# Low parts last: reordering the products of a split-precision trunk step on one Trainium2 core

## The chip, the cores and the metric

The kernel runs on one core of one Trainium2 chip. The metric is the device time of one execution in microseconds; smaller is better. Six instruction streams matter. PE (TensorE) multiplies matrices; PEld, its weight load, is listed beside it. DVE (VectorE), ACT (ScalarE) and POOL (GpSimd) work on elements. SP (SyncE) issues most of the DMAs, and POOL issues those that accumulate into their destination.

## The reference, cut to what matters

One step of a decoder layer for 512 prompt positions and 8 sample positions (520 columns in all), model width 1024, everything in float32:

```
h = x + 0.5 * swiglu(rms_norm(x), gate1, up1, down1)          # first FFN, 2816 wide
proj = rms_norm(h) @ w_in                                     # -> pool input, z, x/B/C, dt
pool_out = windowed means of the pool input, mixed by w_pool
y = ssd_scan(silu(conv(x/B/C)), dt)                           # 4 chunks of 128 positions, 16 heads
y = group_norm((y + d_skip * x) * silu(z)) * ssd_norm         # 2 groups of heads
h = h + concat(pool_out, y) @ w_out                           # 1536 -> 1024
h = h + 0.5 * swiglu(rms_norm(h), gate2, up2, down2)          # second FFN
out = rms_norm(h)
```

For the 8 samples the scan is one step from a given state: the new state is the old one times a decay plus an outer product, and the sample's output needs, for each of 16 heads, the old state multiplied by the C row and summed over its 128 columns. That sum is called a **readout** here.

## The kernel before, in words

**Split precision.** A float32 matmul is replaced by three faster ones. Every weight tile and every activation tile is held as a high part (rounded) and a low part (the rest): w = whi + wlo, x = xhi + xlo, and w·x is taken as whi·xhi + whi·xlo + wlo·xhi. The helper mm3 (L145) issues these three for one block of 128 rows: L146 (whi, xhi), L149 (whi, xlo), L150 (wlo, xhi). A product over 512 or 1024 rows is 4 or 8 calls of mm3 that accumulate into one PSUM bank. So the low weight is used by the third matmul of a product already.

**Making the parts.** load_unit (L140) loads a raw weight by SP's queue; split (L129) makes the high part by an ACT cast (L134) and the low part by a DVE subtraction, raw minus high (L136). The other way is part_by_dma (L230): ACT casts the high part, ACT writes its negative into the low tile (L232), and a DMA from POOL's queue adds the raw weight from DRAM (L233). In the second FFN the load of a tile does the same in L380 to L382, and the quarter of a tile that the code calls qs goes through part_by_dma. Raw tiles, high and low tiles and PSUM banks rotate through a few buffers, so an early release of one lets a later load begin.

**The FFNs** (class Ffn). A fast scheme forms a block of outputs from seven products instead of eight; each product (method product, L448) is four mm3 calls (j = 0 to 3) into a bank called A or BE. Tiles whose names begin with Down are the down projection in the same scheme, and their activations are called gs. The first matmul of a product is pinned in program order; everything else is placed by a list scheduler that simulates the program when the kernel is built (L1405) and fixes the order of each engine's instructions.

**The mixer.** Its order is written out by hand as strings: CONV_PLAN, GATE_PLAN, LAST_PLAN (L41 to L48), in which a letter is a stage and a number its argument. In GATE_PLAN: z are eight units of the z projection; A and B are the two halves of one scan block (numbers 0 to 7: four chunks for each of two head groups); s is a number of sample readouts; G(g) (gate, L1249) multiplies head group g by silu(z), and needs that group's readouts; H(g) (gate_out, L1261) squares the result on ACT, sums the squares on DVE (L1268), sums over partitions on PE into psr_y (L195), takes root and reciprocal, and writes the normalised activations catg (L1276 to L1278). o, g, h (wout, L1232) are the units of the out projection for the pooled part, head group 0 and head group 1: four units each, with four mm3 calls for each of four banks, and DVE adds each bank to h (L1243).

A sample readout (sample, L1088) covers one sample and one group of heads: SP loads a C row (cb, L1090) and a 128 x 4 x 128 state (h0, L1092, four buffers), DVE multiplies them (L1094, pinned), and four ACT instructions with an accumulator output (L1097, pinned) sum 128 columns each. There are 16 of them. The states themselves are updated later, during the second FFN (L1139 to L1143).

Of the kernel before, what the change touches and what calls it, by code (L numbers as in the profile page):

```python
# [13 lines left out]
ALU = mybir.AluOpType  # L14
# [8 lines left out]
HB = NT // 2  # L23
HALVES = (slice(0, HB), slice(HB, NT))
KD = D // P
# [9 lines left out]
CHUNKS = (8, 8, 6)  # L35
LOW_ON_DVE = ((2, 0), (3, 0), (KF - 1, 1))
ON_ACT = 4
STATES = ((1, 1, 1, 1), (6, 17, 19, 20, 21), 4)
LOW_BY_DMA = {1: (2, 3, 4, 5, 6), 2: (*range(7), 9, 11)}

CONV_PLAN = (  # L41
    "b0 b1 d0 b2 b3 x0 x1 v0 d1 x2 x3 d2 X0 p0 y0 c0 A0 k0 p1 x4 m0 x5 B0 c1 p2 m1 A1 x6 c2 A2 B1 x7 X1 m2 A3"
)
GATE_PLAN = (
    "z0 B2 A4 z1 B3 p3 s1 z2 B4 s2 z3 c3 A5 s2 s2 z4 m3 B5 s2 A6 z5 e0 s2 G0 z6 A7 s2 z7 B6 s2 o0 H0 o1 B7 s1 G1 o2 "
    "o3 g0 g1 H1 g2 g3"
)
LAST_PLAN = "h0 h2 h1 n0 h3 n1 n2 n3"  # L48
# [15 lines left out]
def tile_trunk_step(ctx: ExitStack, tc: tile.TileContext, ins: dict, outs: dict):  # L64
    nc = tc.nc
# [6 lines left out]
    wp = ctx.enter_context(tc.tile_pool(name="wp", bufs=3, side="right"))  # L72
    tmp = ctx.enter_context(tc.tile_pool(name="tmp", bufs=2, side="right"))
    dr = ctx.enter_context(tc.tile_pool(name="dr", bufs=1, space=DRAM))
    ps = [None]
# [5 lines left out]
    vec = vx[:, :NVEC]  # L81
    h = vx[:, NVEC:].rearrange("p (d t) -> p d t", d=KD)
# [62 lines left out]
    def mm3(ps, whi, wlo, xhi, xlo, start, stop, pin=False, **kw):  # L145
        first = nc.tensor.matmul(ps, whi, xhi, start=start, stop=False, **kw)  # L146
        if pin:
            tc.keep_in_program_order(first)
        nc.tensor.matmul(ps, whi, xlo, start=False, stop=False, **kw)  # L149
        nc.tensor.matmul(ps, wlo, xhi, start=False, stop=stop, **kw)  # L150

    def ws(w, k, m=P):
        return w[:, k * m : (k + 1) * m]
# [76 lines left out]
    def part_by_dma(hi, lo, s, home):  # L230
        nc.scalar.copy(hi, s)
        nc.scalar.activation(out=lo, in_=hi.bitcast(F32), func=AF.Copy, scale=-1.0)  # L232
        nc.gpsimd.dma_start(out=lo, in_=home, accum_op=ALU.add)  # L233
# [22 lines left out]
    class Ffn:  # L256
# [175 lines left out]
        def quarter(self, f):  # L432
# [7 lines left out]
            if len(src.shape) == 3:  # L440
                h, l = (t.rearrange("p (j c) -> p j c", j=4) for t in (hi, lo))
            if f in LOW_BY_DMA[self.i] and (f, 1) not in LOW_ON_DVE:
                part_by_dma(h, l, src, self.dram[f][1][:, 512:])
# [4 lines left out]
        def product(self, f, p):  # L448
            js = range(KD // 2)
            if f not in self.A:  # L450
                self.load(f, *self.behind.get(f, ((), (), False)))
                n = f"{self.i}_{f}"
                self.A[f] = ps[0].tile([P, 512], F32, tag="A", bufs=2, name=f"A{n}")
                self.BE[f] = ps[0].tile([P, 2, 512], F32, tag="BE", bufs=2, name=f"BE{n}")
                self.ac[f] = [self.wx.tile([P, 2, HB], F32, tag="ac", bufs=3, name=f"ac{n}_{q}") for q in range(2)]
            if p != 1 and 4 not in self.w[f]:
                self.quarter(f)
            slot, dst, opens = {1: (0, 0, True), 2: (1, 1, True), 5: (3, 2, True), 6: (5, 0, False),
                                3: (2, 2, False), 7: (4, 0, False), 4: (6, 0, False)}[p]
            opens = opens and (p != 2 or f in self.whole)  # L460
            out = self.A[f] if dst == 0 else self.BE[f][:, dst - 1]
            (whi, wlo), k = self.w[f][p]
            xth, xtl = self.nx[:2]
            for j in js:
                if isinstance(f, int):
                    x = xth[:, j, slot], xtl[:, j, slot]
                else:
                    x = (self.gs[f.c * CHUNKS[0] // 2 + j][:, q, {5: 6, 6: 5}.get(slot, slot)] for q in range(2))
                mm3(out[:, :HB], ws(whi, k[j]), ws(wlo, k[j]), *x, opens and j == 0,
                    j == KD // 2 - 1, pin=j == 0 and (self.i == 1 or f != 1), skip_group_check=True)  # L470
            a, c = self.ac[f]
            if p == 1 and f not in self.whole:
                a = self.BE[f][:, :, :HB]
            keep = {1: a[:, 0], 6: a[:, 1], 7: c[:, 0], 5: c[:, 1]}.get(p)
            if keep is not None:
                self.copied = nc.scalar.copy(keep, out[:, :HB]).ins  # L476
                if (f, p) == (2, 7):
                    self.tail = self.copied
            if p == 7:
                nc.vector.tensor_tensor(out=c[:, 0], in0=c[:, 0], in1=c[:, 1], op=ALU.add)  # L480
# [53 lines left out]
        def stream(self, before, last_chunk):  # L534
# [6 lines left out]
            for t in tiles:  # L541
                for _ in range(STATES[0][t.d] if not isinstance(t, int) else t in STATES[1]):
                    next(self.states, None)
# [68 lines left out]
        def down_by_half(self, c, lo, after, wd):  # L612
            n = KF - lo
            banks, units = {}, []
            for d in range(KD):
                if d < STATES[2]:
                    next(self.states)
# [104 lines left out]
    nx2, xa = [], []  # L722
# [51 lines left out]

    ps[0] = tc.alloc_tile_pool(name="ppm", bufs=8, space=PSUM, reuse_waits="tile")
    mixer(tc, ins, outs, dict(locals()))
    f2["xg"].release()
    xa[0].release()
# [69 lines left out]
def mixer(tc, ins, outs, e):  # L848
    nc = tc.nc
    cst, act, wp, tmp, dr, pool = (e[x] for x in ("cst", "act", "wp", "tmp", "dr", "pool"))  # L850
    ones, queued, squared = e["ones"], e["queued"], tuple(e["added"])
    bank, load_unit, mm3, ws, v, rstd, rstds, vec, h, nx2, raw_tile, open_f2, fin, fill = (
        e[x] for x in ("bank", "load_unit", "mm3", "ws", "v", "rstd", "rstds", "vec", "h", "nx2", "raw_tile",
                       "open_f2", "fin", "fill"))
    xh, xl, _, r = nx2[0]
    xa = e["xa"][0]
# [194 lines left out]
    ysm = mp.tile([P, NX, NS], F32, tag="ysm", name="ysm")  # L1051
# [4 lines left out]
    def rows_bc(b, a, g):  # L1056
        return scr_bc.rearrange("b (a g n) -> b a g n", a=2, g=2)[b, a, g].unsqueeze(0).to_broadcast([P, P])
# [27 lines left out]
        nc.vector.tensor_tensor(out=sxdt[:, gs], in0=sdt[:, gs], in1=X[:, gs, SEQ:NT], op=ALU.mult)  # L1085


    def sample(b, g):  # L1088
        cb = tmp.tile([P, HB], F32, tag="ta", name=f"cb{b}{g}")[:, :P]
        nc.sync.dma_start(out=cb, in_=rows_bc(b, 1, g))  # L1090
        h0 = mp.tile([P, 4, P], F32, tag="h0", bufs=4, name=f"h0_{b}{g}")
        nc.sync.dma_start(out=h0, in_=ins["state_ssm"][:, b, 4 * g : 4 * g + 4])  # L1092
        tc.keep_in_program_order(
            nc.vector.tensor_tensor(out=h0, in0=h0, in1=cb.unsqueeze(1).to_broadcast([P, 4, P]), op=ALU.mult))  # L1094
        for q in range(4):
            tc.keep_in_program_order(
                nc.scalar.activation(out=junk, in_=h0[:, q], func=AF.Copy,  # L1097
                                     accum_out=ysm[:, 4 * g + q, b : b + 1]))
# [131 lines left out]
            nc.vector.tensor_tensor(out=zbox[0][:, j, hs], in0=bs[b][:, :HB], in1=r[:, hs], op=ALU.mult)  # L1230

    def wout(cat, j, d2, fin=None):  # L1232
        wh, wl = load_unit(ins["w_out"][j, d2], 1024, f"wo{j}{d2}", behind.get((j, d2), ()))
        for d in (2 * d2, 2 * d2 + 1):
            for b, hs in enumerate(HALVES):
                if d != 1 or j != 2:
                    ps = bank(f"wo{j}_{d}{b}")
                else:
                    ps = e["ps"][0].tile([P, 512], F32, tag="A", bufs=2, name=f"wo{j}_{d}{b}")
                for k in range(4):  # L1240
                    i = (d % 2) * 4 + k
                    mm3(ps[:, :HB], ws(wh, i), ws(wl, i), cat[:, 0, k, hs], cat[:, 1, k, hs], k == 0, k == 3)
                nc.vector.tensor_tensor(out=h[:, d, hs], in0=ps[:, :HB], in1=h[:, d, hs], op=ALU.add)  # L1243
                if fin is not None:
                    fin(d, b, hs)

    cats, behind = {}, {}
# [35 lines left out]

    smp = [(b, g) for g in range(2) for b in range(NS)]

    def samples(n):
        for _ in range(n):
            if smp:
                sample(*smp.pop(0))

    pooled, box = [], {}

    def ssd(c):
        return c % NC, c // NC

    def outs_a():
# [14 lines left out]
        "c": lambda j: pooled[j][0](),  # L1311
        "m": lambda j: pooled[j][1](),
        "s": samples,
        "A": lambda j: ssd_a(*ssd(j)),
        "B": lambda j: ssd_b(*ssd(j)),
        "z": zproj,
        "o": lambda j: wout(catp, 0, j),
        "G": gate,
        "H": gate_out,
        "g": lambda j: wout(cats[0], 1, j),  # L1320
        "h": lambda j: wout(cats[1], 2, j, fin),
        "n": fill,
        "e": lambda j: outs_a(),
# [101 lines left out]
```

## Time and profile before

| | us |
|---|---|
| three runs of the kernel | 962.70, 962.92 (median), 964.66 |
| the profiled execution | 963.72 |
| its span, first to last instruction | 961.9 |
| PE busy / DVE busy / ACT busy / POOL busy | 945.5 / 852.3 / 641.2 / 144.9 |

The mean granted clock of TensorE was 0.996. By stage, on the profile's clock: the first FFN runs to about 355 us, the mixer from there to about 615 (in it the out projection from 526 to 611, its last units mixed with the start of the second FFN), the second FFN to 942, the final norm to the end.

How to read a row of the timeline: start and duration in us, engine, line of the kernel, operation, output tile, an arrow, the input tiles, the shapes, the count; in brackets the idle time of the engine before it and what ended that. A matmul's own duration (0.28 us) is longer than its distance from the next one, because they overlap in the array. A row of waits gives the waiting engine, tile and line, what it waited for, the total in us, how often, and the longest. A row of stretches gives the stretch, its length, and then the busy time (and the number of instructions) of PE, PEld, DVE, ACT and POOL, the granted clock, the share of the DMA engines and GB/s.

### The profile page before, as it was taken

How to read it: one execution, taken by the hardware profiler on the slowest of the kernel's cores; microseconds unless marked ns; L12 is line 12 of the kernel's file. 1: busy time of each engine (PE TensorE's matmuls, PEld its weight loads, DVE VectorE, ACT ScalarE, POOL GpSimd, SP SyncE). 2: the span in 40 equal slices, each digit the busy share in tenths (PEclk: the TensorE clock that was granted, in tenths of full speed). 3: DMA queues.
4: the chain of work that ended last, by engine and by line, in shares of the span. 5: the costliest groups of instructions: out<-in, count | busy, mean ns of one | idle time of the engine just before them, and what ended most of it. 6: DMA issues, size and time to landing. Idle time of an engine off the chain costs nothing. (4 is left out here: it accounts for less than half of the span.)

```text
span 961.9 us, 19663 instructions
## 1 busy us (share of the span) xinstructions
PE 945.5 (98%) x7652; PEld 926.2 (96%) x7652; DVE 852.3 (89%) x1460; ACT 641.2 (67%) x1208; POOL 144.9 (15%) x228
## 2 busy tenths in 40 slices
PE   9999999999999999999999999999999999999996
PEld 8999999999999999999999999999999999999995
DVE  6999899998988788779979998898889999989886
ACT  7777756677566455485688645777776676766763
POOL 0011100001000001046252000112112101122120
PEclk9999999999999999999999999999999999999998
DMA  7665553455544243363355323457666646666642
GB/s 210 181 166 149 142 165 112 123 147 141 159 123 115 87 133 101 93 195 117 111 157 166 108 89 121 110 126 171 166 154 188 160 126 155 174 176 175 185 144 90
DMA packets 53629, 137.29 MB, mean 143 GB/s; under 512 B 7640, under 2 KB 15768, under 8 KB 53536
## 3 DMA queue, kind: packets, MB, share of 16 engines
q1 hardware_dynamic: 39840, 104.18, 33.6%
q0 software_dynamic: 13424, 31.73, 17.2%
q8 instruction: 60, 0.98, 0.4%
q14 instruction: 33, 0.27, 0.1%
q10 hardware_dynamic: 272, 0.13, 0.0%
HBM read 128.67 MB, written 7.34 MB: 141 GB/s over the span
## 5 line engine op out<-in xcount | busy, mean ns | idle before, releaser
L476 ACT COPY ac<-A 128x260 f32<-128x260 f32 x85 | 31.7, 373 | 34.7 <-PE A L150 33.5
L412 DVE TENSOR_TENSOR s<-raw 128x1024 f32<-128x1024 f32 x39 | 47.6, 1220 | 3.6 <-DMA raw<-in_w2gu 2.5
L476 ACT COPY ac<-BE 128x260 f32<-128x260 f32 x41 | 15.4, 376 | 30.0 <-PE BE L150 29.0
L146 PE MATMUL inx<-xh_mx,whi_inx 128*128 128x260 f32 x112 | 31.8, 284 | 0.0
L149 PE MATMUL inx<-xl_mx,whi_inx 128*128 128x260 f32 x112 | 31.6, 282 | 0.0
L150 PE MATMUL inx<-xh_mx,wlo_inx 128*128 128x260 f32 x112 | 31.6, 282 | 0.0
L977 DVE SCALAR_TENSOR_TENSOR A<-U,h,A 128x544 f32<-128x544 f32 x36 | 28.8, 799 | 1.1 <-ACT A L975 0.7
L295 PE MATMUL P<-x,raw 128*128 128x260 f32 x128 | 28.9, 387 | 0.0
L295 PEld LDWEIGHTS P<-x,raw 128*128 128x128 f32 x128 | 24.6, 193 | 4.0 <-DMA raw<-in_w1gu 0.3
L146 PE MATMUL wo<-catg,whi_wo 128*128 128x260 f32 x96 | 27.6, 287 | 0.0
L134 ACT CAST thi<-raw 128x1024 fp32r<-128x1024 f32 (+1 forms) x14 | 14.2, 1012 | 20.0 <-PE wo L149 9.9
L150 PE MATMUL wo<-catg,wlo_wo 128*128 128x260 f32 x96 | 27.2, 283 | 0.0
L149 PE MATMUL wo<-catg,whi_wo 128*128 128x260 f32 x96 | 27.1, 282 | 0.0
L1097 ACT ACTIVATE junk<-h 128x128 f32<-128x128 f32 x64 | 19.7, 308 | 7.9 <-DVE h L1094 6.5
L150 PE MATMUL A<-xth_f,qs 128*128 128x260 f32 x84 | 24.0, 286 | 0.9 <-DMA qs<-in_w2gu 0.8
L1139 ACT ACTIVATE so<-br,sxdt 128x128 f32<-128x128 f32 x64 | 22.5, 375 | 3.3 <-DVE room L1141 3.1
L146 PE MATMUL A<-xth_f,qs 128*128 128x260 f32 x84 | 23.9, 284 | 0.0
L149 PE MATMUL A<-xtl_f,qs 128*128 128x260 f32 x84 | 23.7, 282 | 0.0
L237 DVE TENSOR_TENSOR gs<-gq,gs 128x780 fp32r<-128x780 f32 (+1 forms) x28 | 23.2, 829 | 0.4 <-ACT gs L236 0.4
L146 PE MATMUL inz<-xh_mx,whi_inz 128*128 128x260 f32 x80 | 22.9, 287 | 0.0
L149 PE MATMUL inz<-xl_mx,whi_inz 128*128 128x260 f32 x80 | 22.7, 284 | 0.0
L150 PE MATMUL inz<-xh_mx,wlo_inz 128*128 128x260 f32 x80 | 22.6, 283 | 0.0
(2530 smaller groups left out, 4747.3 us busy)
## 6 DMA issues: line engine op xcount, KB each, us to landing
raw<-in_w2gu SPq DMA_DIRECT2D x44, 512.0 KB, 4.2
raw<-in_w1gu SPq DMA_DIRECT2D x41, 512.0 KB, 4.1
raw<-in_w_in SPq DMA_DIRECT2D x24, 512.0 KB, 3.6
raw<-in_w1d SPq DMA_DIRECT2D x16, 512.0 KB, 4.3
raw<-in_w2d SPq DMA_DIRECT2D x16, 512.0 KB, 4.6
raw<-in_w_out SPq DMA_DIRECT2D x12, 512.0 KB, 3.6
ab<-scr_acs SPq DMA_DIRECT2D x8, 512.0 KB, 4.5
h<-in_state_ssm SPq DMA_DIRECT2D x16, 256.0 KB, 3.5
```

Source lines behind the costliest of these rows:

```text
L134: cast = nc.scalar.copy(h, src)
L146: first = nc.tensor.matmul(ps, whi, xhi, start=start, stop=False, **kw)
L149: nc.tensor.matmul(ps, whi, xlo, start=False, stop=False, **kw)
L150: nc.tensor.matmul(ps, wlo, xhi, start=False, stop=stop, **kw)
L237: low = nc.vector.tensor_tensor(out=lo, in0=s, in1=hi.bitcast(F32), op=ALU.subtract)
L295: mm = nc.tensor.matmul(self.banks[f, u][b][:, :HB], ws(self.raw[f][:, u], j + 4 * q), xg[:, slot[q]], start=j == q == 0, stop=j == 3 and ...
L412: nc.vector.tensor_tensor(out=s1, in0=diag, in1=up0, op=ALU.add)
L476: self.copied = nc.scalar.copy(keep, out[:, :HB]).ins
L977: nc.vector.scalar_tensor_tensor(out=A[:, :n], in0=U[:, j : j + n], scalar=w(j), in1=A[:, :n], op0=ALU.mult, op1=ALU.add)
L1097: nc.scalar.activation(out=junk, in_=h0[:, q], func=AF.Copy, accum_out=ysm[:, 4 * g + q, b : b + 1]))
L1139: nc.scalar.activation(out=o[:, q], in_=br, func=AF.Copy, scale=sxdt[:, j, b : b + 1]))
```

## The change

Four edits.

1. A new helper, mm_low_last, issues for one product all whi·xhi and whi·xlo matmuls first (eight of a product of twelve) and the four wlo·xhi behind them. The products of the second FFN's tiles and all out units use it; the first FFN, the in projection and the last down projection keep mm3.
2. The low parts of the out units g0 and g1 (OUT_LOW_BY_DMA) are made by part_by_dma instead of a DVE subtraction.
3. The first four sample readouts (r2, r2) are summed by one DVE reduction each instead of four ACT instructions.
4. In GATE_PLAN the readouts stand earlier: two instead of one after p3, and the last one, which stood between B7 and G1, is gone from there. B7 goes ahead of o1.

```diff
+OUT_LOW_BY_DMA = ((1, 0), (1, 1))
 GATE_PLAN = (
-    "z0 B2 A4 z1 B3 p3 s1 z2 B4 s2 z3 c3 A5 s2 s2 z4 m3 B5 s2 A6 z5 e0 s2 G0 z6 A7 s2 z7 B6 s2 o0 H0 o1 B7 s1 G1 o2 "
+    "z0 B2 A4 z1 B3 p3 r2 z2 B4 r2 z3 c3 A5 s2 s2 z4 m3 B5 s2 A6 z5 e0 s2 G0 z6 A7 s2 z7 B6 s2 o0 H0 B7 o1 G1 o2 "
     "o3 g0 g1 H1 g2 g3"
 )
...
+    def mm_low_last(ps, whi, wlo, xhi, xlo, start, pin=False, **kw):
+        for k, w in enumerate(whi):
+            for x in (xhi[k], xlo[k]):
+                mm = nc.tensor.matmul(ps, w, x, start=start, stop=False, **kw)
+                if pin:
+                    tc.keep_in_program_order(mm)
+                start = pin = False
+        for k, w in enumerate(wlo):
+            nc.tensor.matmul(ps, w, xhi[k], start=False, stop=k == len(wlo) - 1, **kw)
...
@@ product
+            if self.i == 2:
+                mm_low_last(out[:, :HB], wh, wl, *xs, opens, pin, skip_group_check=True)
+            else:
+                for j in js:
+                    mm3(out[:, :HB], wh[j], wl[j], xs[0][j], xs[1][j], opens and j == 0, j == js[-1],
+                        pin=pin and j == 0, skip_group_check=True)
...
@@ sample
+        if reduce:
+            tc.keep_in_program_order(
+                nc.vector.tensor_reduce(out=ysm[:, 4 * g : 4 * g + 4, b], in_=h0, axis=mybir.AxisListType.X, op=ALU.add))
+            return
...
@@ wout
-        wh, wl = load_unit(ins["w_out"][j, d2], 1024, f"wo{j}{d2}", behind.get((j, d2), ()))
+        src, name = ins["w_out"][j, d2], f"wo{j}{d2}"
+        if (j, d2) in OUT_LOW_BY_DMA:
+            raw = raw_tile(name)
+            nc.sync.dma_start(out=raw, in_=src)
+            wh, wl = e["weight_homes"](1024, name, wp, 3, ("whi", "wlo"))
+            e["part_by_dma"](wh, wl, raw, src)
+        else:
+            wh, wl = load_unit(src, 1024, name, behind.get((j, d2), ()))
...
-                for k in range(4):
-                    i = (d % 2) * 4 + k
-                    mm3(ps[:, :HB], ws(wh, i), ws(wl, i), cat[:, 0, k, hs], cat[:, 1, k, hs], k == 0, k == 3)
+                i = range((d % 2) * 4, (d % 2) * 4 + 4)
+                mm_low_last(ps[:, :HB], *([ws(w, k) for k in i] for w in (wh, wl)),
+                            *([cat[:, q, k, hs] for k in range(4)] for q in range(2)), True)
...
+        "r": lambda n: samples(n, True),
```

More of the change, by code (lines that the diff above doesn't have):

```diff
@@ L463, in product @@
             xth, xtl = self.nx[:2]
[L464 to L470, printed above, removed]
+            if isinstance(f, int):
+                xs = [[x[:, j, slot] for j in js] for x in (xth, xtl)]
+            else:
+                u = {5: 6, 6: 5}.get(slot, slot)
+                xs = [[self.gs[f.c * CHUNKS[0] // 2 + j][:, q, u] for j in js] for q in range(2)]
+            wh, wl = ([ws(w, k[j]) for j in js] for w in (whi, wlo))
+            pin = self.i == 1 or f != 1
+            if self.i == 2:
[4 more added lines that the diff above has]
+                        pin=pin and j == 0, skip_group_check=True)
             a, c = self.ac[f]
@@ L851, in mixer @@
     ones, queued, squared = e["ones"], e["queued"], tuple(e["added"])
-    bank, load_unit, mm3, ws, v, rstd, rstds, vec, h, nx2, raw_tile, open_f2, fin, fill = (
-        e[x] for x in ("bank", "load_unit", "mm3", "ws", "v", "rstd", "rstds", "vec", "h", "nx2", "raw_tile",
+    bank, load_unit, mm3, mm_low_last, ws, v, rstd, rstds, vec, h, nx2, raw_tile, open_f2, fin, fill = (
+        e[x] for x in ("bank", "load_unit", "mm3", "mm_low_last", "ws", "v", "rstd", "rstds", "vec", "h", "nx2", "raw_tile",
                        "open_f2", "fin", "fill"))
@@ L1085, in sample_x, with sample @@
         nc.vector.tensor_tensor(out=sxdt[:, gs], in0=sdt[:, gs], in1=X[:, gs, SEQ:NT], op=ALU.mult)
-    def sample(b, g):
+    def sample(b, g, reduce):
         cb = tmp.tile([P, HB], F32, tag="ta", name=f"cb{b}{g}")[:, :P]
@@ L1232, in wout @@
     def wout(cat, j, d2, fin=None):
-        wh, wl = load_unit(ins["w_out"][j, d2], 1024, f"wo{j}{d2}", behind.get((j, d2), ()))
+        src, name = ins["w_out"][j, d2], f"wo{j}{d2}"
[4 more added lines that the diff above has]
+            e["part_by_dma"](wh, wl, raw, src)
+        else:
+            wh, wl = load_unit(src, 1024, name, behind.get((j, d2), ()))
         for d in (2 * d2, 2 * d2 + 1):
@@ L1284, in mixer, with samples @@
     smp = [(b, g) for g in range(2) for b in range(NS)]
-    def samples(n):
+    def samples(n, reduce=False):
         for _ in range(n):
-            if smp:
-                sample(*smp.pop(0))
+            sample(*smp.pop(0), reduce)
     pooled, box = [], {}
```

## The prediction, made before the result was known

> **What bounds the kernel now.** I read the page's busy times first, then the stretches, then the waits of TensorE (PE).
>
> ```profile
> span 961.9 us, 19663 instructions
> PE 945.5 (98%) x7652; PEld 926.2 (96%) x7652; DVE 852.3 (89%) x1460; ACT 641.2 (67%) x1208; POOL 144.9 (15%) x228
> ```
>
> PE is busy for 98% of the span and the matmul count doesn't change, so nothing here can be worth more than the time in which PE stands still: 961.9 - 945.5 = 16.4 us.
>
> ```profile
> 100.00:150.00 50.00, 50.00 (x419) 50.00 (x418) 45.55 (x71) 31.75 (x50) 4.30 (x5) 1.00 0.56 151
> ...
> 480.00:510.00 30.00, 29.92 (x254) 27.82 (x253) 22.87 (x47) 24.77 (x80) 12.36 (x12) 1.00 0.56 167
> 510.00:560.00 50.00, 50.00 (x419) 48.02 (x418) 49.69 (x99) 34.53 (x104) 5.89 (x4) 1.00 0.42 133
> ```
>
> Undisturbed, 419 matmuls take 50 us: one starts every 0.12 us, whatever its own duration says. VectorE (DVE, third pair) is idle for 7.1 us of 480 to 510 and for 0.3 us of 510 to 560: there it runs behind PE and works without a gap. The waits of PE say where that or anything else reaches PE:
>
> ```profile
> PE psr_y L195 <- DVE X L1268: 1.5, 1, 1.5
> PE A_Down(c=0, d=1)_8807 L150 <- DMA wlo_Down(c=0, d=1)a<-in_w2d: 1.4, 1, 1.4
> ...
> PE A L150 <- DMA qs<-in_w2gu: 0.8, 1, 0.8
> ...
> PE A L150 <- DMA qlo_4b<-in_w1gu: 0.6, 1, 0.6
> PE A_Down(c=1, d=2)_10486 L150 <- DMA wlo_Down(c=1, d=2)a<-in_w2d: 0.6, 1, 0.6
> PE A L150 <- DVE slo_17d L136: 0.5, 1, 0.5
> ```
>
> L150 is the matmul that takes the low part of a weight. Four of these waits are for a low part in the second FFN, which the change reorders; qlo_4b is in the first FFN, which it doesn't. psr_y is gate_out(1) waiting for DVE in the mixer. These are the targets.
>
> **The change part by part. Low parts last.** One stall close up:
>
> ```profile
> 708.17 0.28 PE L146 MATMUL A_Down(c=0, d=1)_8807<-gs,whi_Down(c=0, d=1)a 128*128 128x260 f32 x1
> 708.29 0.28 PE L149 MATMUL A_Down(c=0, d=1)_8807<-gs,whi_Down(c=0, d=1)a 128*128 128x260 f32 x1
> 709.94 0.39 PE L150 MATMUL A_Down(c=0, d=1)_8807<-gs,wlo_Down(c=0, d=1)a 128*128 128x260 f32 x1 [1.37 <-DMA wlo_Down(c=0, d=1)a<-in_w2d]
> 710.16 0.28 PE L146 MATMUL A_Down(c=0, d=1)_8807<-gs,whi_Down(c=0, d=1)a 128*128 128x260 f32 x1
> ...
> 751.83 0.28 PE L149 MATMUL A<-xtl_f,qs 128*128 128x260 f32 x1
> 752.19 0.39 PE L150 MATMUL A<-xth_f,qs 128*128 128x260 f32 x1
> ```
>
> The low weight is wanted by the third matmul of the product. The slip is 709.94 - 708.29 - 0.12 = 1.53 us and 0.10 in the step behind it, 1.63 in all, so a wait of the table costs about 0.25 more than it says; 752.19 slips by 0.24 + 0.10 and isn't even listed. Afterwards eight matmuls stand ahead of the first low one instead of two: it is wanted 6 x 0.12 = **0.71 us later**. The number of matmuls, and of changes of weight (8 in 12), stays. Each stall gives at most 0.71: 709.94 (1.63) gives 0.71; qs at 668.9 (0.8 + 0.25) gives 0.71; 752.19 gives all of its 0.34; 842.7 (0.6 + 0.25) and 868.3 (0.5 + 0.25) give 0.71 each if independent. But the chain that ended last goes between these two over a state's DMA and DVE, not over PE:
>
> ```profile
> 844.26 4.05 DMA room<-in_state_ssm
> ```
>
> Time gained at 842.7 doesn't move what 868.3 waits for, so I count the two once. Sum: 0.71 + 0.71 + 0.34 + 0.71 = **2.5 us**; bounds 0.7 (one gain, the others hanging on the same late chain) and 3.2 (all five).
>
> The order has a price at the start of that FFN, where x is late:
>
> ```profile
> 617.18 0.97 DVE L237 TENSOR_TENSOR xtl_f<-xg_f,xth_f 128x780 fp32r<-128x780 f32 x1
> 618.07 1.24 DVE L237 TENSOR_TENSOR xtl_f<-xd_f,xth_f 128x1040 fp32r<-128x1040 f32 x1
> ...
> 618.86 0.28 PE L149 MATMUL A<-xtl_f,whi_1a 128*128 128x260 f32 x1
> ...
> 619.36 0.39 PE L149 MATMUL BE<-xtl_f,shi_1c 128*128 128x260 f32 x1
> ```
>
> DVE delivers x's low parts of the last j at 618.1 (for A) and 619.3 (for BE), and PE takes BE's at once. BE has then done ten of its twelve matmuls, since the low weights of the first three j don't need that x. With all four low ones last it has done seven: 3 x 0.12 = 0.36 us of work no longer lies beside the wait. I charge **+0.4** (bounds 0, if other ready matmuls fill the place, and 0.7, if A loses its three as well). The other products of both FFN stages want x 0.36 us earlier, where no wait of the table is for x: nothing, bound +0.3.
>
> **Out units.** For g0 and g1 the low part leaves DVE; the same stretch shows what waits for it:
>
> ```profile
> 545.64 1.22 DVE L136 TENSOR_TENSOR wlo_wo<-raw,whi_wo 128x1024 fp32r<-128x1024 f32 x1
> ...
> 551.99 1.22 DVE L136 TENSOR_TENSOR wlo_wo<-raw,whi_wo 128x1024 fp32r<-128x1024 f32 x1
> ...
> 554.18 0.69 DVE L1094 TENSOR_TENSOR h<-h,cb 128x512 f32<-128x512 f32 x1
> ...
> 565.22 0.69 DVE L1268 TENSOR_TENSOR X<-X 128x520 f32<-128x520 f32 x1
> ...
> 564.32 0.28 PE L150 MATMUL wo<-catg,wlo_wo 128*128 128x260 f32 x1
> 566.05 1.11 PE L195 MATMUL psr_y<-X,ones 128*128 128x260 f32 x4 [1.45 <-DVE X L1268]
> ```
>
> DVE has no gap from 510 until the L1268 that PE waits for. Out of this stretch go two L136 (1.13 from start to start) and the last sample's L1094 (0.60), which moves up with its two DMAs: 2.9 us. PE stands 566.05 - 564.32 - 0.12 = 1.6 us. So the wait goes, **-1.6**, if DVE doesn't come later to 510; PE's own work is late next. Added are two ACT negations and two POOL DMAs:
>
> ```profile
> 547.25 1.05 ACT L134 CAST whi_wo<-raw 128x1024 fp32r<-128x1024 f32 x1 [1.33 <-PE wo L149]
> ...
> 558.80 0.28 PE L149 MATMUL wo<-catg,whi_wo 128*128 128x260 f32 x1
> ...
> 700.75 1.05 ACT L381 ACTIVATE wlo_Down(c=0, d=1)a<-whi_Down(c=0, d=1)a 128x1024 fp32r<-128x1024 f32 x1
> ...
> 702.10 0.88 POOL L382 DMA_DIRECT2D wlo_Down(c=0, d=1)a<-in_w2d  x1 [11.20 <-ACT wlo_Down(c=0, d=1)a L381]
> ...
> 594.14 0.90 POOL L233 DMA_DIRECT2D qs<-in_w2gu  x1 [53.46 <-DVE h L1243]
> ```
>
> g1's cast at 547.25, a negation of 1.05, and a DMA that in the same form was in PE's hands 709.94 - 702.10 = 7.8 us after its issue: about 557.4. PE starts g1 at 558.7 and wants the low part 0.95 us on, at 559.6. Cost nothing, margin 2.2 us. POOL has 53 us without other work, so nothing queues behind these DMAs; ACT has 15 us free in 510 to 560. Without that cover each us of lateness is a us.
>
> **Samples.** Four readouts leave ACT for DVE:
>
> ```profile
> L1097 ACT ACTIVATE junk<-h x64: 291/310/314, 485.6 to 556.3; 128x128 f32<-128x128 f32 x64
> L1097 ACT ACTIVATION_READ_ACCUMULATOR junk<-h x64: 185/187/197, 485.8 to 556.5; 128x1 f32 x64
> ...
> L199 DVE RECIPROCAL yr<-yr x4: 1720/1748/1779, 538.0 to 569.0; 128x260 f32<-128x260 f32 x4
> ...
> SPq L1092 <- ACT junk L1097: 16.2, 11, 3.9
> ```
>
> ACT loses 16 pairs of at most 0.50 us, 8 us. DVE gets four reductions of 128x512, an operation the trace doesn't have: from 0.60 (the multiply L1094 of that shape, start to start) to 3.4 us (a reciprocal's 1.75 us for 260 elements, scaled). I take 0.60, since a reduction reads the tile once as L1094 does: 2.4 us, and 0.6 for the moved multiply, 3.0 us inside the 7.1 us that DVE idles in 480 to 510. State loads on SP's queue waited 16.2 us for ACT's readouts to free their buffers; that shrinks, and so may DVE's idle time. Cost 0, bound +3.0 on DVE if none of that idle time can be used.
>
> **B7 ahead of o1.** It issues no more, only 5.9 us earlier, at 532.5 when gate_out(0)'s sums are done:
>
> ```profile
> 531.77 0.68 DVE L1215 TENSOR_TENSOR hst<-pst,hst 128x512 f32<-128x512 f32 x1
> ...
> 532.51 0.47 PE L146 MATMUL wo<-catp,whi_wo 128*128 128x260 f32 x1
> ```
>
> The state that it reads is ready at 532.45: nothing, bound +0.7 (one more DVE operation ahead). It lets the gate's DVE work start sooner.
>
> **The sum.** -1.6 - 2.5 + 0.4 = **-3.7 us**. The profiled execution took 963.72 us around its span of 961.9: 960.0. The median of the three runs, 962.92, lies 0.8 below it, so **959.2 us** is predicted.
>
> **Rivals.** (1) The FFN gains don't reach the end: PE arrives earlier, DVE and the DMAs don't, and the stalls reappear one product on. For: DVE is without a gap around several stalls. Against: their chains start at matmuls of the tile before. Time: 962.9 - 1.6 + 0.4 = 961.7. (2) Slower: the reductions make DVE late. They lengthen the gapless stretch that gate_out(1) ends. Per reduction r, DVE comes 4r + 0.6 later less the idle time it can use (0 to 7.1), less 2.9; PE's wait there grows by that much, and the kernel is slower than before once it exceeds the 2.1 us that the second FFN gives. The point is 4r + 0.6 less the usable idle time = 5.0, that is r = 1.1 (none usable) or 2.9 (all). At r = 3.4 and all usable the growth is 4 x 3.4 + 0.6 - 7.1 - 2.9 = 4.2: 962.9 + 4.2 - 2.1 = 965.0. Against: L1094's row. (3) POOL's DMAs starve under a DVE without gaps. If they had to wait for DVE's next pause, at 566, the low parts would land near 573 instead of 557, 13 us after they are wanted: about 962.9 + 13 - 2.1 = 974. Against: the DMA of 702.10 took 0.88 us to issue and 7.8 to land:
>
> ```profile
> 700.00:705.00 5.00, 4.91 (x41) 4.70 (x40) 5.00 (x10) 3.64 (x10) 0.88 (x1) 1.00 0.42 107
> ```
>
> with DVE busy for 5.00 of those 5 us. This is a rule of the Trainium skill ("SBUF — State Buffer", "SBUF: two separate sides"): descriptors that GpSimd writes wait while a VectorE operation holds the port that they share. By that rule it would be 974. The trace doesn't bear it out for these VectorE operations. (4) The scheduler orders the lists anew and the intended order doesn't come out: about 962.9, either way.
>
> **Chances.** Forecast 0.58, (1) 0.18, (2) 0.09, (3) 0.04, (4) 0.11. A measurement can tell 0.2%, 1.9 us, from no change. Faster by more, below 961.0: the forecast, a third of (1), a third of (4): 0.68. Within: 0.17. Slower: 0.15. The low end takes all five stalls, the mixer and no charge: 962.9 - 1.6 - 3.2 - 0.6 (small slips such as 752.19's that no row lists) = 957.5, rounded down to 957.0; the high end goes into (2), at a loss of 0.5 us: 963.4.
>
> **What would show it.** Right: no psr_y wait; first low matmul ninth in its product, the four L150 waits at most their old value less 0.71; a longer wait for xtl_f at 619; reductions of 0.6 to 0.7 us. Wrong: a wait of PE for wlo_wo from in_w_out, a psr_y wait that grows, or as much total waiting in the second FFN with other names.

## The result, and the profile after

| | us |
|---|---|
| before, six runs | 962.81 (959.27 to 964.66) |
| after, six runs | 956.34 (955.96 to 958.85) |
| ratio, 95% interval | 0.9942 (0.9929 to 0.9955) |
| profiled execution, before and after | 963.72, 956.44 |

By the ratio the change takes off 5.6 us (4.3 to 6.8). 959.2 was predicted, from 957.0 to 963.4: the sign holds, the gain is larger, and the median lies 0.7 below the low end; by the ratio, which puts the 962.92 that I started from at 957.3, it lies just inside. One execution of a later kernel, neither, took 5284 us and is left out of its row. In the lines below, every line number behind the new helper has moved: L150 is now L151, and in the new order a high matmul is L156 and a low one L161.

First the page of the changed kernel, its busy times:

```profile
span 954.7 us, 19636 instructions
PE 942.1 (99%) x7652; PEld 925.0 (97%) x7652; DVE 854.0 (89%) x1462; ACT 635.7 (67%) x1178; POOL 148.9 (16%) x230
```

The span is 7.2 us shorter, with as many matmuls. PE's idle time fell from 16.4 to 12.6 us. The other 3.4 us came out of its busy time, which the page gives as 942.1 instead of 945.5 for the same matmuls: the records of neighbours overlap, and a slip that only shortens the overlap isn't idle time. So the idle time that I took as the limit of the gain wasn't one. Second, the waits of PE that the view of the waits lists, but for two at the start and the end of the kernel (for eps 1.1, for sq_last 0.6) that were there before:

```profile
PE BE_Down(c=1, d=1)_10344 L156 <- ACT c_Down(c=1, d=1)_1_10346 L493: 1.3, 1, 1.3
...
PE BE L156 <- ACT BE L493: 0.7, 1, 0.7
```

psr_y is gone, and so are all four waits for a low part in the second FFN. No wait is for a weight any more. Two new ones are for copies that ACT makes (L493). Third, where the stages begin, by the same instructions in PE's timeline. Of before:

```profile
355.91 0.38 PE L195 MATMUL psr_mx<-acc_mx,ones 128*128 128x260 f32 x1
...
607.45 0.28 PE L146 MATMUL A<-xth_f,whi_1a 128*128 128x260 f32 x1
...
942.24 0.38 PE L824 MATMUL psl<-acc_last,ones 128*128 128x260 f32 x1
```

and of after:

```profile
355.13 0.38 PE L206 MATMUL psr_mx<-acc_mx,ones 128*128 128x260 f32 x1
...
604.20 0.28 PE L156 MATMUL A<-xth_f,whi_1a 128*128 128x260 f32 x1
...
935.13 0.38 PE L841 MATMUL psl<-acc_last,ones 128*128 128x260 f32 x1
```

psr_mx begins the mixer, whi_1a the second FFN, and psl comes behind it; each of the two stretches holds as many matmuls after as before (2050 and 2709). The first FFN, whose code is the same, is 0.8 us shorter: the wait for qlo_4b (0.6) isn't there in this execution. With that code unchanged it ends between 354.7 and 356.3 in the profiles of all kernels here. The mixer fell from 251.5 to 249.1 us (2.5), the second FFN from 334.8 to 330.9 (3.9). The three together give 7.1.

Fourth, the stretches of after that answer to those of before (PE, PEld, DVE, ACT, POOL):

```profile
480.00:510.00 30.00, 30.00 (x256) 28.14 (x255) 26.01 (x50) 20.57 (x56) 14.98 (x12) 1.00 0.62 188
510.00:560.00 50.00, 50.00 (x419) 48.02 (x418) 50.00 (x99) 37.66 (x100) 6.86 (x5) 1.00 0.49 136
```

DVE took 3.14 us more in 480 to 510 (26.01 against 22.87) and was still idle for 4.0 of 30. In 510 to 560 it works without a gap as before, but further ahead, as its timeline shows:

```profile
482.04 0.68 DVE L1111 TENSOR_TENSOR h<-h,cb 128x512 f32<-128x512 f32 x1
482.76 0.69 DVE L1114 TENSOR_REDUCE ysm<-h 128x4 f32<-128x512 f32 x1
483.36 1.20 DVE L1111 TENSOR_TENSOR h<-h,cb 128x512 f32<-128x512 f32 x1
...
558.52 0.70 DVE L1296 TENSOR_TENSOR X<-X 128x520 f32<-128x520 f32 x1
...
563.02 1.04 PE L206 MATMUL psr_y<-X,ones 128*128 128x260 f32 x4
```

The reduction takes 0.60 us from its start to the next (482.76 to 483.36), as the multiply of before did. The sum that PE waits for (L1296) is done at 559.2; before it began at 565.22. PE wants it at 563.02: 3.8 us to spare instead of a wait. The low part of an out unit, by DMA from POOL:

```profile
545.30 0.90 POOL L244 DMA_DIRECT2D wlo_wo<-in_w_out  x1 [11.61 <-ACT wlo_wo L243]
549.20 0.85 POOL L244 DMA_DIRECT2D wlo_wo<-in_w_out  x1 [3.00 <-ACT wlo_wo L243]
```

and the same two in the view of the DMAs, with the KB of each and the median us from issue to landing (its last number):

```profile
wlo_wo<-in_w_out POOLq DMA_DIRECT2D x2, 512.0 KB, 5.8
```

Issue takes 0.85 to 0.90 us and landing 5.8, while DVE is busy for 50.00 of 50 us. PE waits for neither.

Last, the product that stood for 1.63 us in the prediction's stall, now:

```profile
695.94 0.88 POOL L393 DMA_DIRECT2D wlo_Down(c=0, d=1)a<-in_w2d  x1 [10.29 <-PE A L161]
...
702.71 1.11 PE L156 MATMUL A_Down(c=0, d=1)_8797<-gs,whi_Down(c=0, d=1)a 128*128 128x260 f32 x8
...
703.65 0.65 PE L161 MATMUL A_Down(c=0, d=1)_8797<-gs,wlo_Down(c=0, d=1)a 128*128 128x260 f32 x4
```

The first low matmul is the ninth, 0.94 us behind the first high one, and doesn't wait. The DMA is issued 6.8 us ahead of the product's first matmul. Before, it was issued at 702.10 and the product began at 708.17, 6.1 ahead. So the low part is wanted 0.7 us later and is also under way 0.7 earlier, together 1.4, a little less than the 1.53 that PE stood there. The rest is the DMA itself, here in before and in after:

```profile
wlo_Down(c=0, d=1)a<-in_w2d POOLq DMA_DIRECT2D x1, 512.0 KB, 7.8
...
wlo_Down(c=0, d=1)a<-in_w2d POOLq DMA_DIRECT2D x1, 512.0 KB, 6.4
```

At 6.4 us it landed at 702.3, ahead of the product's first matmul: in this execution the old order would hardly have waited either. What the order does shows better at the wait for qs at 668.9. That DMA took 8.1 us to land before and 8.2 in after, and PE no longer waits for it:

```profile
656.42 0.86 POOL L244 DMA_DIRECT2D qs<-in_w2gu  x1 [0.49 <-ACT qs L243]
...
664.73 0.71 PE L161 MATMUL A<-xth_f,qs 128*128 128x260 f32 x4
```

PE takes the low part 8.31 us behind the issue. Before, the DMA was issued at 660.73 and PE was ready for the low part at 667.95, 7.22 behind. Of these 1.09 us the order gives 0.71, an earlier issue the rest.

### The profile page after: what moved, and what is told of

The parts are those of the page before. It is cut to its first block, busy times and chain, and to the rows that moved or that the text cites. A ratio compares the mean times of both kernels' runs of the same rounds, so it can differ in the third digit from the quotient of the medians.

```text
span 954.7 us, 19636 instructions
## 1 busy us (share of the span) xinstructions
PE 942.1 (99%) x7652; PEld 925.0 (97%) x7652; DVE 854.0 (89%) x1462; ACT 635.7 (67%) x1178; POOL 148.9 (16%) x230
## 5 line engine op out<-in xcount | busy, mean ns | idle before, releaser
L493 ACT COPY ac<-A 128x260 f32<-128x260 f32 x85 | 31.7, 373 | 37.2 <-PE A L161 18.5
L493 ACT COPY ac<-BE 128x260 f32<-128x260 f32 x41 | 15.4, 377 | 35.2 <-PE BE L161 16.9
L150 PE MATMUL inx<-xl_mx,whi_inx 128*128 128x260 f32 x112 | 31.6, 282 | 0.0
L151 PE MATMUL inx<-xh_mx,wlo_inx 128*128 128x260 f32 x112 | 31.6, 282 | 0.0
L156 PE MATMUL wo<-catg,whi_wo 128*128 128x260 f32 x192 | 27.4, 285 | 0.0
L156 PEld LDWEIGHTS wo<-catg,whi_wo 128*128 128x128 f32 x192 | 24.8, 188 | 0.2
L1271 DVE TENSOR_TENSOR h<-wo,h 128x260 f32<-128x260 f32 x48 | 19.2, 422 | 5.0 <-PE wo L161 4.8
L150 PE MATMUL inz<-xl_mx,whi_inz 128*128 128x260 f32 x80 | 22.7, 284 | 0.0
L151 PE MATMUL inz<-xh_mx,wlo_inz 128*128 128x260 f32 x80 | 22.6, 283 | 0.0
L147 PEld LDWEIGHTS inx<-xh_mx,whi_inx 128*128 128x128 f32 x112 | 21.1, 188 | 0.2 <-issue 0.2
L156 PE MATMUL A<-xth_f,qs 128*128 128x260 f32 x84 | 21.2, 283 | 0.0
L156 PE MATMUL A<-xtl_f,qs 128*128 128x260 f32 x84 | 21.2, 284 | 0.0
L151 PEld LDWEIGHTS inx<-xh_mx,wlo_inx 128*128 128x128 f32 x112 | 21.1, 188 | 0.0
```

What stands on the lines that cost most here:

```text
L156: mm = nc.tensor.matmul(ps, w, x, start=start, stop=False, **kw)
```

## The experiments

**What another execution of before shows.** The kernel before, profiled once more:

> The kernel before, profiled a second time. Theory (a part of the stalls that I summed belongs to the one profiled execution, whose 963.72 us lie above the middle of the runs): psr_y's 1.5 us is there again, since VectorE's work sets it, but the waits for qs and wlo_Down change by up to a us each, and the span is 1 to 3 us shorter. Rival (all seven are fixed by the schedule): the same rows within 0.2 us.

961.71 us, span 959.9. Its waits of PE, the first and last that matter:

```profile
PE psr_y L195 <- DVE X L1268: 1.5, 1, 1.5
...
PE BE_Down(c=0, d=3)_9075 L146 <- ACT BE_Down(c=0, d=3)_9075 L476: 0.6, 1, 0.6
PE A L150 <- DVE slo_17d L136: 0.5, 1, 0.5
PE A_Down(c=1, d=2)_10486 L146 <- ACT c_Down(c=1, d=2)_0_10488 L476: 0.4, 1, 0.4
...
PE A L150 <- DMA qs<-in_w2gu: 0.2, 1, 0.2
```

The wait for psr_y and that for slo_17d, both for DVE, come back to a tenth. The largest wait for a DMA, 1.4 us for wlo_Down, isn't there (the DMA landed after 6.3 us), and that for qs is 0.2 instead of 0.8. This execution's mixer takes 251.6 us as before, its second FFN 333.25, 1.5 less. So the two largest stalls that I counted in the second FFN differ from one execution to the next, and others come in their place: 0.6 and 0.4 us for copies on ACT, of the kind that seemed new in after.

**The two places apart.** ffn2_only keeps the new order for the products of the second FFN alone (no low parts by DMA, the old GATE_PLAN, mm3 in the out units). mixer_only is the changed kernel but for this:

```diff
-            if self.i == 2:
+            if False:
                 mm_low_last(out[:, :HB], wh, wl, *xs, opens, pin, skip_group_check=True)
```

> Only the products of the second FFN take low parts last; the plan, the readouts and the out units are those of before. Theory (two separate gains): the L150 waits of the second FFN go as in the changed kernel, about -3.5 us there, and the psr_y wait of 1.5 us stays: 959.3. Rival 1 (my forecast's size): each stall gives at most 0.71, -2.1: 960.7. Rival 2 (the stalls went because the mixer ends earlier and the scheduler places the loads of the second FFN otherwise): the same number of stalls under other names, 962.5.

> The changed kernel with the old order (high, high, low for each j) in the second FFN's products; the mixer is that of the changed kernel. Theory: no psr_y wait, PE reaches the second FFN about 2.5 us earlier than before and the L150 waits (qs, wlo_Down, slo_17d; about 4.5 us with their slips) are back: 960.0. Rival 2: the L150 waits stay away because the mixer did it: 956.5.

| | us, median | ratio, 95% interval | mixer | second FFN |
|---|---|---|---|---|
| ffn2_only | 959.17 | 0.9977 (0.9963 to 0.9991) | 251.1 | 331.0 |
| mixer_only | 959.75 | 0.9975 (0.9962 to 0.9988) | 250.4 | 332.85 |
| after | 956.34 | 0.9942 (0.9929 to 0.9955) | 249.1 | 330.9 |

(The stages are measured in the profiled executions, between the same three instructions as above.) Each place gives about 0.24%, 2.2 and 2.4 us, and 4.6 in sum; after's 5.6 agrees within the intervals. The rival, that PE's gain in the FFN only shifts the stalls, would have left ffn2_only at the time of before. It falls, by a narrow margin. ffn2_only came out at the 959.3 that its theory had, but as a gain (before ran at 961.65 beside it) its 2.2 us are nearer to the first rival's 2.1, the forecast's size, than to the theory's 3.5. The waits of ffn2_only show what each edit does:

```profile
PE psr_y L206 <- DVE X L1296: 1.5, 1, 1.5
PE BE_Down(c=1, d=1)_10354 L156 <- ACT c_Down(c=1, d=1)_1_10356 L493: 1.3, 1, 1.3
...
PE BE L156 <- DVE xtl_f L248: 0.2, 1, 0.2
PE A_Down(c=1, d=1)_10353 L161 <- DMA wlo_Down(c=1, d=1)a<-in_w2d: 0.2, 1, 0.2
```

psr_y stays, the low parts are hardly waited for, and the wait for xtl_f that the prediction charged 0.4 us for is 0.2. In mixer_only psr_y is gone and waits for low parts are back (qs 0.6, wlo_Down 0.4).

**The other order.** low_first issues the four low matmuls of a product ahead of the eight high ones, in the second FFN:

```diff
-                mm_low_last(out[:, :HB], wh, wl, *xs, opens, pin, skip_group_check=True)
+                mm_low_first(out[:, :HB], wh, wl, *xs, opens, pin, skip_group_check=True)
```

> The changed kernel with the four low products first in the second FFN: the low weight is wanted 0.24 us earlier than before the change and 0.95 us earlier than with it, the high weight 0.48 us later. Theory (what counts is when the low part is wanted): the L150 waits of before come back, each 0.24 us longer, and small ones join them at other tiles; 3 to 6 us more than the changed kernel, 959.5 to 962.5. Rival (what counts is that the high part or x is wanted at another time, or that high and low are apart): no more waits than in the changed kernel, 956.3.

964.41 us, ratio 1.0022 (1.0009 to 1.0036), 8 us above after. The sign is the theory's, the size isn't: I had expected at most 962.5. The rows are from its slowest execution, 966.8.

```profile
PE BE L165 <- ACT BE L503: 2.7, 2, 2.5
PE A L165 <- DVE slo_9d L137: 1.7, 1, 1.7
PE A L165 <- DVE slo_19d L137: 1.3, 1, 1.3
...
PE A_Down(c=1, d=2)_10476 L165 <- DVE slo_Down(c=1, d=2)d L137: 0.6, 1, 0.6
```

L165 is the low matmul there. What comes late is hardly a DMA (0.4 us in all) but the subtractions on DVE, 3.6 us in the three rows, and one copy on ACT. So here the order within a product decides whether DVE's queue is on the path. The run also pins a low matmul instead of a high one as the first of each product; how much of the 8 us comes of that, it doesn't show.

**The order in other stages.** ffn1_too uses mm_low_last in the first FFN as well; wout_mm3 is the changed kernel with mm3 in the out units.

```diff
-            if self.i == 2:
+            if True:
```

> The changed kernel with low parts last in the first FFN as well. Theory: the one wait for a low part there (qlo_4b, 0 to 0.85 us from execution to execution) goes, nothing else waits there: 955.7 to 956.3. Rival (its x is made late at the start, 34 us, and low parts last take work from beside that): up to 0.4 us more, 956.7.

> The changed kernel with the old order of products in the out units alone. Theory (no wait of before was for a low part of an out unit): the time of the changed kernel within 0.5 us, 956.3 to 956.8, psr_y not waited for. Rival (low parts last is what keeps g0's and g1's DMAs from being waited for): a wait for wlo_wo of up to 0.7 us each, 957 to 958.

ffn1_too: 958.31 us, ratio 0.9952 (0.9936 to 0.9968), no better than after and above the 956.7 of either expectation. There is no wait for qlo_4b, but there was none in after's execution either, and two others come:

```profile
PE A_Down(c=0, d=0)_1184 L156 <- DVE gs L248: 1.1, 1, 1.1
...
PE A L156 <- DVE sq L545: 0.7, 1, 0.7
```

Low parts last puts the high matmuls of all four j ahead, so the last activation is wanted earlier, and the first row is for such an activation (gs). The second is for the release of bank A, which a multiplication on DVE (L545) still has to read. So where an activation or a bank is late, the order can cost what it gains. wout_mm3: 958.47 us (I had expected at most 956.8), 0.9954 (0.9936 to 0.9971), mixer 250.0 us. The view lists no wait for psr_y and none for an out unit's weight. Its interval overlaps after's, so the order in the out units is worth between nothing and about 2 us; the mixer's 0.9 us between two profiled executions says little, since mixer_only, with after's own code there, took 250.4.

**What removes the wait for psr_y.** Four kernels, each the changed one with one or two of the mixer's edits undone: no_dma_low (OUT_LOW_BY_DMA empty), old_plan (the old GATE_PLAN: one readout later, all on ACT, o1 ahead of B7), neither (both), o1_first (o1 ahead of B7 alone).

```diff
-OUT_LOW_BY_DMA = ((1, 0), (1, 1))
+OUT_LOW_BY_DMA = ()
...
-    "z0 B2 A4 z1 B3 p3 r2 z2 B4 r2 z3 c3 A5 s2 s2 z4 m3 B5 s2 A6 z5 e0 s2 G0 z6 A7 s2 z7 B6 s2 o0 H0 B7 o1 G1 o2 "
+    "z0 B2 A4 z1 B3 p3 s1 z2 B4 s2 z3 c3 A5 s2 s2 z4 m3 B5 s2 A6 z5 e0 s2 G0 z6 A7 s2 z7 B6 s2 o0 H0 o1 B7 s1 G1 o2 "
```

> The changed kernel with g0's and g1's low parts made on VectorE again. Theory (in the changed kernel the last sum of gate_out(1) ends at 559.2 and PE comes for it at 563.0, so 2.3 us more on VectorE still fit): no psr_y wait, the time of the changed kernel, 956.3 to 956.8. Rival (the forecast's sum, in which those 2.3 us are most of the 2.9 that cover the wait): a psr_y wait of 0.5 to 1.6 us comes back, 957 to 958.

> The changed kernel with the old hand-written order: readouts on ScalarE, the last one between B7 and G1, o1 ahead of B7; low parts last and the two DMAs stay. Theory (the order is what lets the gate's VectorE work start early; two subtractions less are 2.3 us and cover 1.6): psr_y wait 0 to 0.5 us, 956.5 to 957. Rival (the order alone made the room): the psr_y wait is back at 1 us or more, 957.5 to 958.

> The changed kernel with the old GATE_PLAN and without the two low parts by DMA; low parts last stays in the second FFN and in the out units. Theory: each of the two edits alone covers the wait for psr_y, so without both it is back at 1.2 to 1.6 us and the time is 1.5 us above the changed kernel's, about 957.9. Rival: low parts last in the out units already gives DVE the time that it lacked, no wait for psr_y above 0.3, about 956.5.

> The changed kernel with o1 ahead of B7 again. Theory: the place of B7 is worth nothing, the time is within 0.5 us of the changed kernel's and psr_y isn't waited for. Rival: with B7 later gate(1) starts later on DVE and psr_y is waited for again, 0.3 to 1 us.

| | us, median | ratio, 95% interval | wait for psr_y | mixer |
|---|---|---|---|---|
| no_dma_low | 956.82 | 0.9942 (0.9921 to 0.9963) | 0.2 | 249.5 |
| old_plan | 956.61 | 0.9945 (0.9923 to 0.9967) | none | 249.6 |
| o1_first | 957.05 | 0.9949 (0.9932 to 0.9966) | none | 249.5 |
| neither | 958.65 | 0.9968 (0.9952 to 0.9983) | 1.3 | 251.0 |

```profile
PE psr_y L206 <- DVE X L1296: 1.3, 1, 1.3
```

That row is of neither: with both undone the wait is back, and the time is 2.5 us above after's by the ratios (in the profiled executions 2.0 in the mixer and 1.4 in the second FFN). With either one, the wait is gone or nearly so. The two are cover for the same 1.5 us and don't add. The place of B7 is worth nothing that can be measured.

**The reductions.** act_readouts has the readouts at their new places, but all on ACT:

```diff
-        "r": lambda n: samples(n, True),
+        "r": lambda n: samples(n),
```

> The changed kernel with all readouts summed on ACT, at their new places. Theory: the four reductions lie in DVE's idle time and ACT had time for its own, so neither way matters: within 0.5 us of the changed kernel's time, no wait for psr_y. Rival: ACT's readouts hold SP's state loads back, DVE's multiplications come later and psr_y is waited for again, up to 1 us.

958.08 us, ratio 0.9966 (0.9954 to 0.9978), 2.3 us above after. Neither theory had it: psr_y isn't waited for, PE waits 1.9 us in the z projection instead.

```profile
484.86 0.29 ACT L1118 ACTIVATE junk<-h 128x128 f32<-128x128 f32 x1
...
488.19 1.03 ACT L135 CAST thi<-raw 128x1024 fp32r<-128x1024 f32 x1
...
489.26 2.17 DVE L137 TENSOR_TENSOR tlo<-raw,thi 128x1024 fp32r<-128x1024 f32 x1 [2.60 <-ACT thi L135]
...
505.34 0.69 DVE L1111 TENSOR_TENSOR h<-h,cb 128x512 f32<-128x512 f32 x1 [2.95 <-DMA cb<-scr_bc]
505.95 0.42 DVE L1251 TENSOR_TENSOR zs<-inz,r_mx 128x260 f32<-128x260 f32 x1
...
506.42 0.39 PE L147 MATMUL inz<-xh_mx,thi 128*128 128x260 f32 x1 [1.89 <-DVE zs L1251]
```

The same steps in the changed kernel:

```profile
484.98 1.05 ACT L135 CAST thi<-raw 128x1024 fp32r<-128x1024 f32 x1 [0.47 <-PE inz L150]
...
486.97 1.21 DVE L137 TENSOR_TENSOR tlo<-raw,thi 128x1024 fp32r<-128x1024 f32 x1
...
502.41 0.69 DVE L1111 TENSOR_TENSOR h<-h,cb 128x512 f32<-128x512 f32 x1 [1.92 <-DMA cb<-scr_bc]
503.02 0.42 DVE L1251 TENSOR_TENSOR zs<-inz,r_mx 128x260 f32<-128x260 f32 x1
```

Eight pairs of ACT instructions, two readouts, stand ahead of the cast of a weight: it comes 3.2 us later, DVE idles for it, everything on DVE behind it is 2.3 to 2.9 us late, and with it the release of PE's bank (zs). The last link is a DMA: zs stands behind a readout's multiply that waits for its C row, 2.95 us instead of 1.92. SP issues the rows due then from 501.48 on instead of 499.58, behind waits for DVE. So moving readouts up pays here only if they leave ACT.

**The new waits.** PE's wait of 1.3 us at 832 is for a copy on ACT. In the changed kernel's timeline of ACT:

```profile
831.50 0.37 ACT L1160 ACTIVATE so<-br,sxdt 128x128 f32<-128x128 f32 x1 [3.29 <-DVE room L1162]
831.81 0.37 ACT L493 COPY c_Down(c=1, d=1)_1_10346<-BE_Down(c=1, d=1)_10344 128x260 f32<-128x260 f32 x1
```

The copy is queued behind a state update, which waits 3.29 us for DVE. so_ahead issues the four ACT operations of an update first and DVE's four behind them:

```diff
+            for q in range(4):
+                j = 4 * g + q
                 tc.keep_in_program_order(
                     nc.vector.scalar_tensor_tensor(out=hs[:, q], in0=hs[:, q], scalar=sdec[:, j, b : b + 1],
```

> The changed kernel, but for one state update ACT issues its four outer products ahead of DVE's four updates, instead of one by one. Theory: what PE waits 1.3 us for at 832 is ACT, whose copies are queued behind an outer product that waits for DVE; with that wait gone the time falls by 0.8 to 1.5 us, to 954.8 to 955.6. Rival: the copies are as late for another reason, or the next product waits instead: 956.3.

958.29 us, ratio 0.996 (0.9946 to 0.9975): not faster than after. Both waits for copies are gone, as the theory had it, and the rival's half is true as well:

```profile
PE A L161 <- DVE slo_17d L137: 0.9, 1, 0.9
...
PE A L161 <- DVE slo_9d L137: 0.3, 1, 0.3
```

DVE's timeline of the same kernel shows part of why:

```profile
860.42 0.85 DVE L1164 SCALAR_TENSOR_TENSOR room<-room,sdec,so 128x128 f32<-128x128 f32 x3
861.19 1.22 DVE L137 TENSOR_TENSOR slo_17d<-raw,shi_17d 128x1024 fp32r<-128x1024 f32 x1
```

Three updates in a row, free to run together now, stand ahead of the low part of slo_17d, which began at 857.26 in the changed kernel. They are 0.85 us of that delay of 3.9. Its cast on ACT (shi_17d) also begins 1.5 us later, at 857.53 instead of 856.06, and the rest isn't taken apart. The wait moved from a copy on ACT to a subtraction on DVE; the second FFN of the profiled execution is 0.4 us shorter than after's.

## Why the prediction was right in sign and too small

*The wait for psr_y goes, -1.6.* Right; its cause is shown by the run called neither. The working was one-sided: I added up what leaves DVE as if all of it were needed, but either edit alone covers the wait (DVE is 3.8 us ahead now).

*Samples, cost 0.* The size was right: 0.60 us per reduction, and the 3.14 us on DVE lie in its idle time as worked out (3.0). The reason was incomplete. I asked only what the reductions cost DVE and how long SP's loads wait for ACT. What is queued behind the readouts on ACT, the casts of weights, I left out, and act_readouts shows that to be worth 2.3 us at the new places.

*The mixer in all.* I let the wait for psr_y stand for the whole of it, 1.6 us. Between the stage's first and last instruction the pair before and after gives 2.5, but part of that is scatter. Four profiled executions with the wait (before, before_again, ffn2_only, neither) take 251.0 to 251.6 us; eight with 0.2 of it or none (all but act_readouts, with its own wait, and low_first, whose stages mix otherwise) take 249.1 to 250.4, in the mean 1.8 less. In the pair, 0.7 of the other 0.9 us are two slips: for px on ACT at 466.8 (0.4), and at the z unit of 504.97 (0.3), whose bank DVE frees behind a readout's multiply that waits 2.56 us for its C row. Both stand in before and before_again; ffn2_only, with the mixer of before, hasn't the first, and neither, with the old plan, hasn't the second. So 1.6 was about right.

*Low parts last, -2.5, and +0.4 at the start.* By ffn2_only 2.2 us (0.9 to 3.6) against a forecast of 2.1. That agreement is luck, for the terms were not right. Between profiled executions the stage gains 3.9 us against before and 2.3 against before_again, and that is what is left after the two waits for copies on ACT, 1.3 and 0.7, which I hadn't seen. With the 0.25 that a wait costs more than its row says, they take 2.5. So 4.9 to 6.4 us were gained where I had summed 2.5. The step that was mis-sized is the cap of 0.71 per stall. DMAs are also issued earlier, 0.7 us at wlo_Down and 0.4 at qs; the stalls at 842.7 and 868.3, which I counted once, both went (0.6 us each, when the matmul of the same number is compared in the traces of before and after); and small slips went that no row lists. One term was of its execution alone: the 1.63 us at wlo_Down hung on a DMA of 7.8 us that took 6.3 and 6.4 in before_again and after. The charge of 0.4 appears as a wait of 0.2 in ffn2_only and as none in after.

*POOL's DMAs.* Not starved: 0.90 us to issue and 5.8 to land under a DVE that is busy for 50.00 of 50 us. The Trainium skill ("SBUF — State Buffer", "Who interferes with whom") says as much of these operations: a subtraction or a reduction, unlike a copy, doesn't hold the port on which GpSimd writes descriptors; for the subtraction it calls the reason inferred. The trace agrees for the operations with two inputs that stood on DVE during the two issues, TENSOR_TENSOR (L1271) and SCALAR_TENSOR_TENSOR (L1243, L1306); no reduction did. The rival that I gave 0.04 took the rule without this part.

*Base and range.* I took 0.8 us off for the profiled execution and started at 962.92, which agrees with the 962.34 of the kernel before over 27 runs. By the median the range missed by 0.7: its low end summed five known stalls and one wait, and gave 0.6 to all that no row lists. Of the 1.9 us between the forecast gain (3.7) and the measured (5.6), the profiled executions put 0.2 into the mixer and 0.5 into the second FFN, which takes 333.6 us in the mean of three without the new order there and 331.05 in nine with it (so_ahead and low_first aside), 2.6 less instead of 2.1. The other 1.2 stay open: the interval of each ratio is 1.2 us or more to either side.

## What to carry to other kernels

Where a product accumulates several terms and one operand is made last, issue the terms that need it last: it costs no instruction and gives its makers the time of the others. Check the other operands, since the ones that are now wanted earlier become the next wait (ffn1_too), and count small slips as well as listed waits. For work that moves to an earlier place, ask what stands behind it in its engine's queue: eight pairs of short ACT instructions ahead of one cast cost 2.3 us here, no less than the wait that the move was to remove. And compare more than the total with the forecast: here two errors in the second FFN, a gain too small and a loss left out, cancelled.

## What the runs showed of the hardware

A sum of 128x512 to 128x4 on DVE takes 0.69 us, 0.60 from start to start, as long as the multiply of that shape (0.68). I had bounded it at 3.4. The same sum by four pairs of ACT instructions took 1.7 us: two readouts took 3.3 in act_readouts. The DMA that adds a raw weight of 512 KB onto the low part of wlo_Down(c=0, d=1) took 7.8, 6.3 and 6.4 us to land in three executions. So of the waits for a DMA that one profile shows, several are of that execution only (wlo_Down 1.4 against none, qs 0.8 against 0.2). The waits for DVE in before returned to a tenth of a us, but two for copies on ACT stood in the second execution alone (0.6 and 0.4). Two profiles of the kernel before would have told which stalls to count on.
